# Constants of a one-core hybrid layer are given other sizes, and attention scores are issued without a wait for the low part of k

## The chip, the cores and the metric

One core of a Trainium2 chip runs the kernel. The metric is the device time of one execution in microseconds (us), as a median of several runs. The engines are TensorE (PE in the profile), VectorE (DVE), ScalarE (ACT), GpSimd (POOL) and SyncE (SP), whose queue issues most DMAs. Each works through its own instructions in program order, and semaphores hold an instruction back until its operands are there.

## The reference

A decoder layer on 512 tokens of width 2048, in float32. One input projection feeds two mixers: an RWKV-7 time mixing of 16 heads and an attention of 16 heads of 64, whose three dilated windows are mixed by their softmax denominators. Each branch is gated, then comes one output projection.

```python
h = rms_norm(x, norm_g[l])
proj = jnp.matmul(h, w_in[l]).astype(jnp.float32)
q, k, v, z_att, u_shift, z_rwkv = jnp.split(proj, splits, axis=-1)
att = dilated_mixture_attention(q, k, v, pos) * jax.nn.silu(z_att)
rwk = rwkv7_time_mix(u_shift, z_rwkv, ...) * jax.nn.silu(z_rwkv)
mix = jnp.concatenate([att, rwk], axis=-1).astype(x.dtype)
x = x + jnp.matmul(mix, w_out[l])
return rms_norm(x, final_g)
```

## The kernel before

**The main stream.** The kernel goes through items in a fixed order: the low-rank columns with `k0`; then for each of eight pairs of RWKV heads the columns r, v, z and the next k (`mm_r0`, `mm_v0`, ...); then attention's v (`mv`); q and k of four groups (`mm_qk10` to `mm_qk33`); the gates z8 to z15 (`mm_z8`, ...); at last the output projection (`mo`, `mh`, `mt`). The weights come from HBM into two raw buffers. ScalarE rounds each chunk to a high part (`whi`) and VectorE takes the rest (`wlo`); h is held as `hh` and `hl` in the same way. So every 128 rows of weights are three matmuls of 512 columns: hh by whi, hl by whi, hh by wlo. One item is 48 of them.

**Side work.** All else is written as Python generators, which issue a few instructions and yield a time or the tiles that they want to have ready. `pump` runs between the matmuls of the main stream and resumes those generators whose time has come. A planner (`Model`, `Engine`, `Queue`) keeps a clock of its own by modelled costs, and `wait_for` turns the yielded tiles into a time on it. This happens when the program is built: the result is one fixed order of instructions for each engine, and the chip knows nothing of the planner. One modelled time that moves can thus move all that is placed after it.

**Attention.** q and k of a pair of heads go through a rotation into tiles `m`, whose rows SP's queue collects by eight DMAs of 64 KB into `qa` and eight into `ka`. k is split into `kd` (ScalarE) and `kl` (VectorE). `att` works on units (a pair of heads and a quarter t of the tokens): scores `s` on TensorE (q by kd, then q by kl, for both heads), softmax on VectorE and ScalarE (`ss`, `nm`, `den`), transposes `pt` on TensorE, copied by ScalarE into `pa` and `pb`, and after the last quarter `po`, the product with v. VectorE brings po together with `yl`, the other mixers' part, which is fetched from HBM. The name of a tile counts pair, head and quarter: s400 is pair 4, head 0, quarter 0, and kl_200 belongs to group 2, first pair, head 0, which is pair 4.

**Gates.** `pg` is the product for the gate of one RWKV pair, `gh` and `gl` are its split weights, and `zz`, `zt` and `yl` on VectorE and ScalarE finish it.

**Buffers.** `k2` gives one of 20 buffers of 2 KB, `k4` one of 9 of 4 KB (q and `pa`), `small` a few columns; `cp` holds what stays for the whole kernel. A tile of a pool waits for the last reader of the tile that had the buffer before it. The constants lie below the split weights.

**Start.** `prb` on TensorE spreads the row factors of the norm, from `dg`; `rstd` and `u_lora` on VectorE follow, and the RWKV chain begins there.

Every matmul is recorded at one line, L121, every operation of the other engines at L88, every DMA at L133. So rows are told apart by tiles.

Of the kernel before, what the change touches and what calls it, by code (L numbers as in the profile page):

```python
# [11 lines left out]
F32 = mybir.dt.float32  # L12
F32R = mybir.dt.float32r
I32 = mybir.dt.int32
AF = mybir.ActivationFunctionType
ALU = mybir.AluOpType
# [4 lines left out]
P = 128  # L21
# [11 lines left out]
PV = {}  # L33
# [5 lines left out]
NPV = _o  # L39
# [97 lines left out]
def hymba_kernel(ctx: ExitStack, tc: tile.TileContext, xT, x, wa, wb, wo, pv, w2a2, g2, fg,  # L137
                 cst, rope, amask, bmask, out):
    nc = tc.nc
    ctx.enter_context(tc.manual_schedule())  # L140
    model = Model()
    V = Engine(model, nc.vector, 0.07, 0.00106, 0.18)
    S = Engine(model, nc.scalar, 0.06, 0.00095, 0.25)
# [6 lines left out]
    cp = ctx.enter_context(tc.tile_pool(name="cp", bufs=1))  # L150
    wp = ctx.enter_context(tc.tile_pool(name="wp", bufs=3))
    kp = ctx.enter_context(tc.tile_pool(name="kp", bufs=1))
# [5 lines left out]
    K1N, K2N, K4N, RAWN, AHEAD = 5, 20, 9, 2, 2  # L158

    def k2(shape, name, dt=F32):  # L160
        t = kp.tile([P, 528], dt, tag="k2", bufs=K2N, name=name)
        t = t[:, 0:math.prod(shape[1:])]
        return t if len(shape) == 2 else t.rearrange("p (a b) -> p a b", b=shape[2])

    def k1(shape, name, dt=F32):
        return kp.tile(shape, dt, tag="k1", bufs=K1N, name=name)
# [1 line left out]
    def k4(shape, name, dt=F32):  # L168
        return kp.tile(shape, dt, tag="k4", bufs=K4N, name=name)

    def ps(name, shape=(P, 512)):
        return pp.tile(list(shape), F32, tag="ps", name=name)

    def small(shape, name, bufs=12, dt=F32):
        return sp.tile(shape, dt, tag=f"s{shape[1]}", bufs=4 if shape[1] == 4 else bufs, name=name)

    pvt = cp.tile([P, 112], F32, name="pvt")
    nc.scalar.dma_start(pvt[:, 0:NPV], pv)

    def col(n, i):  # L180
        return pvt[:, PV[n] + i:PV[n] + i + 1]
# [5 lines left out]
    gmask = [csts[:, 320:448], csts[:, 448:576]]  # L187
    bmt = cp.tile([P, 2 * P], F32, name="bmt")
    ones = k2([P, P], "ones")
    V.memset(ones, 1.0)  # L190
    bonesr = cp.tile([P, P], F32R, name="bonesr")
    hw0 = cp.tile([P, 32], F32, name="hw0")
    omu = cp.tile([P, 27], F32, name="omu")
    V.tensor_scalar(omu, pvt[:, 0:27], -1.0, 1.0, ALU.mult, ALU.add)
    warm = small([P, 1], "warm")
    S.activation(warm, ones[:, 0:1], AF.Tanh)

    hth, htl, normed = [], [], []
    rstd = cp.tile([P, T], F32, name="rstd")
    rtok = cp.tile([P, 16], F32, name="rtok")[:, 0:4]  # L200
    xt_b, xq_b, Lb = [], [], []

    def prologue():
        acc = k2([P, T], "acc")
        xs = []

# [49 lines left out]
    def later():  # L256
        bones = k2([P, P], "bones")
        Q.dma_start(bones, cst[:, 576:704])
        Q.dma_start(bmt, bmask)
        yield 1.59, bones  # L260
        V.tensor_copy(bonesr, bones)
        V.tensor_scalar(hw0[:, 0:16], pvt[:, PV["w0"]:PV["w0"] + 16], 0.5, None, ALU.mult)
        V.tensor_scalar(hw0[:, 16:24], pvt[:, PV["k_a"]:PV["k_a"] + 8], -1.0, None, ALU.mult)
        for i in range(2):
            G.memset(xt_b[i], 0.0)
            G.tensor_copy(Lb[i][H[i], :, H[i]], ident[H[i], H[i]][:, None, :].to_broadcast([64, NCH, C]))
            yield 0.5, G
# [136 lines left out]
    def start(gen, *wait, rank=1):  # L404
        sides.append([gen, wait_for(*(wait or (0.0,))), rank])
# [161 lines left out]
    def spill_out(key, t):  # L567
        d = dp.tile([P, T], F32, name=f"sp_{key}")
        Q.dma_start(d, t)
        spill[key] = d  # L570
# [57 lines left out]
    def pre(p, r, k, v):  # L628
# [35 lines left out]
        a = k2([P, T], f"a{p}")  # L664
# [44 lines left out]
        V.tensor_scalar(rn2, rn2, 1e-24, None, ALU.max)  # L709
        V.reciprocal(rn2, rn2)  # L710
        start(subst(p, Mp, rn2), 0.06, Mp, rn2, rank=-1)
        S.activation(a, a, AF.Identity, bias=hw0[:, 16 + p:17 + p], scale=col("k_a", p))
        V.scalar_tensor_tensor(k, a, 1.0, k, ALU.add, ALU.mult)
        rk = k2([P, T], f"rk{p}")
        V.scalar_tensor_tensor(rk, r, col("r_k", p), k, ALU.mult, ALU.mult)
# [212 lines left out]
    def att_mask(t):  # L928
        return (am[0][:, 0:128], am[0][:, 128:384], am[1][:, 0:384], am[2])[t]
# [99 lines left out]
    def two(pa, t):  # L1029
        o = 256 if t == 3 else 0  # L1030
        return pa[:, o:o + 768].rearrange("p (j c) -> p j c", j=2)[:, :, t * P - o:t * P - o + P]

    def att(g):
        units = [(2 * g + pr_, t) for pr_ in range(2) for t in range(4)]
        po, ssb_, pts = {}, {}, {}
        for u in range(len(units) + 2):
            if u < len(units):
                pair, t = units[u]
                while pair not in ready or (t == 0 and u == 0 and pair >= 2 and pair - 1 not in scored):
                    yield 0.5  # L1040
                tl_ = pairs[pair]
                if t == 0:
                    yield 0.1, tl_["q"], tl_["kl", 0], tl_["kl", 1]
                n = max(256, 128 * (t + 1))
                nv = 128 * (t + 1)
                tsl = slice(t * P, (t + 1) * P)
                for h in range(2):
                    sc = ps(f"s{pair}{h}{t}")
                    TE.matmul(sc[:, 0:n], tl_["q"][:, h, tsl], tl_["k", h][:, 0:n], start=True, stop=False)
                    TE.matmul(sc[:, 0:n], tl_["q"][:, h, tsl], tl_["kl", h][:, 0:n], start=False, stop=True)  # L1050
                    ss = k2([P, T], f"ss{pair}{h}{t}")
                    nm = small([P, 1], f"nm{pair}{h}{t}")
                    V.tensor_tensor_reduce(ss[:, 0:nv], sc[:, 0:nv], att_mask(t), -0.125, 3.0e38,
                                           ALU.add, ALU.min, accum_out=nm)
                    den = small([P, 1], f"den{pair}{h}{t}")
                    S.activation(ss[:, 0:nv], ss[:, 0:nv], AF.Exp, bias=nm, scale=-1.0, accum_out=den)
                    ssb_[u, h] = (ss, den)
                if t == 3:
                    scored.add(pair)
            if u >= 2:  # L1060
                pair, t = units[u - 2]
                if t == 3:
                    po[pair] = pm.tile([P, T], F32, tag="mm", name=f"po{pair}")
                    for j in range(4):
                        for h in range(2):
                            hd = (2 * pair + h) * 64
                            pa, pb = pts[pair, h]
                            pj = (pa[:, 0:512], pa[:, 512:896], pb[:, 0:256], pb[:, 256:384])[j]
                            TE.matmul(po[pair][H[h], j * P:T], vt[j][:, hd:hd + 64], pj,
                                      start=(j == 0), stop=(j == 3))  # L1070
                if t == 3:
                    if f"s{pair}" in spill:
                        o = yl.pop(pair)
                        V.tensor_tensor(o, o, po.pop(pair), ALU.mult)
                    else:
                        o = k2([P, T], f"o{pair}")
                        S.copy(o, po.pop(pair))
                    spill_out(f"o{pair}", o)
                elif t == 2 and f"s{pair}" in spill:
                    fetch_y(pair, f"s{pair}")  # L1080
            if 1 <= u <= len(units):
                pair, t = units[u - 1]
                for h in range(2):
                    ss, den = ssb_.pop((u - 1, h))
                    if t == 0:
                        pts[pair, h] = (k4([P, 1024], f"pa{pair}{h}"), k2([P, T], f"pb{pair}{h}"))
                    pa, pb = pts[pair, h]
                    pt = ps(f"pt{pair}{h}{t}")
                    for j in range(t + 1):
                        TE.transpose(pt[:, j * P:(j + 1) * P], ss[:, j * P:(j + 1) * P], ident)  # L1090
                    if t == 0:
                        S.copy(pa[:, 0:P], pt[:, 0:P])
                    else:
                        S.copy(two(pa, t),
                               pt[:, 0:2 * P].rearrange("p (j c) -> p j c", j=2))
                    if t >= 2:
                        S.copy(pb[:, (t - 2) * P:(2 * t - 3) * P], pt[:, 2 * P:(t + 1) * P])
            yield 0.0, S
            if u < len(units):
                for h in range(2):  # L1100
                    ss, den = ssb_[u, h]
                    nv = 128 * (units[u][1] + 1)
                    V.reciprocal(den, den)
                    V.tensor_scalar(ss[:, 0:nv], ss[:, 0:nv], den, None, ALU.mult)
            yield 0.0, V
# [13 lines left out]
    def fetch_y(idx, key):  # L1119
        y = k2([P, T], f"yl{idx}")  # L1120
        Q.dma_start(y, spill[key])
        yl[idx] = y
# [53 lines left out]
            yield 1.05  # L1176

    fgt = []
    ssq = cp.tile([P, 4, 8], F32, name="ssq")
    yt = {}  # L1180

    def residual(nb):
# [247 lines left out]
```

## Time and profile before

| what | value |
|---|---|
| median of 3 runs | 1186.74 us (1185.92 to 1186.84) |
| profiled execution | 1185.99 us, its span 1183.9 us |
| TensorE busy | 1146.4 us, 97% of the span |
| VectorE, ScalarE, GpSimd busy | 62%, 48%, 28% |
| DMA, mean over the span | 118 GB/s, 139.62 MB |

The span runs from the first to the last instruction that the profiler recorded; the execution's own time is 2.1 us longer. TensorE's busy time counts matmuls as they follow one another. A wait of another engine costs only if TensorE waits in the end.

### The profile page before, as it was taken

To read this page: it belongs to the slowest core of one execution; us is meant where nothing else is said; L and a number is where in the kernel's file an instruction comes from. 1 tells how busy PE (TensorE), PEld (TensorE's weight loads), DVE (VectorE), ACT (ScalarE), POOL (GpSimd) and SP (SyncE) were. 2 spreads that over 40 slices of the span, in tenths; PEclk is the share of its full clock that TensorE was granted. 3 is DMA by queue.
4 is the path that set the end of the run, shared out by engine and by line. 5 is a ranking of instruction groups with operands and counts; after the bars stand their busy time and mean duration, and the time that the engine had idled before them with its cause. 6 is when DMAs were issued, how large, how long until landed. Compare 5 with 4: busy or idle time off the path is not lost. (4 is left out here: it accounts for less than half of the span.)

```text
span 1183.9 us, 19123 instructions
## 1 busy us (share of the span) xinstructions
PE 1146.4 (97%) x6878; PEld 938.2 (79%) x6878; DVE 735.2 (62%) x1511; ACT 568.6 (48%) x1254; POOL 336.4 (28%) x586
## 2 busy tenths in 40 slices
PE   7999999999999999999999999999996999999997
PEld 5788777777787777777899977777875778888897
DVE  6667887787767957768743457665655566243252
ACT  6455665645558464564433345544443445232143
POOL 1004885647328470754630001101010000011020
PEclk9999999999999999999999999999998999999999
DMA  7334333242342525234242454433452336444343
GB/s 260 118 92 130 120 105 84 84 126 84 94 136 73 139 65 151 77 100 114 59 121 59 118 166 133 132 109 116 134 142 84 116 113 213 125 125 129 103 125 143
DMA packets 89870, 139.62 MB, mean 118 GB/s; under 512 B 37936, under 2 KB 47664, under 8 KB 89776
## 3 DMA queue, kind: packets, MB, share of 16 engines
q1 hardware_dynamic: 89344, 137.83, 39.1%
q8 instruction: 54, 0.88, 0.3%
q10 hardware_dynamic: 432, 0.58, 0.1%
q14 instruction: 40, 0.33, 0.1%
HBM read 114.44 MB, written 14.75 MB: 109 GB/s over the span
## 5 line engine op out<-in xcount | busy, mean ns | idle before, releaser
L88 POOL TENSOR_TENSOR Xtmp<-XT,Mp 128x248 f32<-128x248 f32 (+30 forms) x248 | 128.9, 520 | 143.6 <-DVE XT L88 112.8
L88 POOL TENSOR_TENSOR XT<-XT,Xtmp 128x248 f32<-128x248 f32 (+30 forms) x248 | 144.6, 583 | 21.4 <-DVE XT L88 2.5
L121 PE MATMUL mm_z<-hh,wlo 128*128 128x512 f32 x256 | 104.1, 407 | 0.0
L121 PE MATMUL mm_z<-hl,whi 128*128 128x512 f32 x256 | 103.2, 403 | 0.0
L121 PE MATMUL mm_qk<-hh,whi 128*128 128x512 f32 x256 | 102.2, 399 | 0.8 <-ACT gtok L88 0.8
L121 PE MATMUL mm_qk<-hl,whi 128*128 128x512 f32 x256 | 102.8, 401 | 0.0
L121 PE MATMUL mm_z<-hh,whi 128*128 128x512 f32 x256 | 102.7, 401 | 0.0
L88 DVE TENSOR_TENSOR wlo<-raw_o,whi 128x512 fp32r<-128x512 f32 x64 | 48.0, 790 | 87.6 <-ACT whi L88 87.6
L121 PE MATMUL mm_qk<-hh,wlo 128*128 128x512 f32 x256 | 102.1, 399 | 0.0
L88 POOL TENSOR_TENSOR y<-y,fg 128x512 f32<-128x512 f32 (+1 forms) x16 | 19.3, 1237 | 272.0 <-ACT mo L88 214.1
L88 ACT ACTIVATE whi<-raw_o 128x512 fp32r<-128x512 f32 x64 | 36.8, 623 | 96.5 <-PE mo L121 73.2
L88 POOL TENSOR_TENSOR m<-m,m 128x512 f32<-128x512 f32 x16 | 22.9, 1451 | 197.7 <-DVE m L88 92.5
L88 ACT ACTIVATE ss<-ss,nm 128x128 f32<-128x128 f32 (+3 forms) x64 | 35.5, 556 | 87.0 <-DVE nm L88 87.0
L121 PE MATMUL mo<-whi,ml 128*128 128x512 f32 x192 | 75.8, 395 | 0.0
L121 PE MATMUL mo<-whi,mh 128*128 128x512 f32 x192 | 75.8, 395 | 0.0
L121 PE MATMUL mo<-wlo,mh 128*128 128x512 f32 x192 | 75.8, 395 | 0.0
L88 DVE TENSOR_TENSOR wlo<-raw_v,whi 128x352 fp32r<-128x352 f32 (+1 forms) x80 | 50.3, 655 | 35.2 <-ACT whi L88 33.9
L88 DVE TENSOR_TENSOR wlo<-raw_z,whi 128x512 fp32r<-128x512 f32 x64 | 48.1, 771 | 33.2 <-ACT whi L88 32.9
L88 DVE TENSOR_TENSOR wlo<-raw_qk,whi 128x512 fp32r<-128x512 f32 x64 | 46.5, 745 | 32.2 <-ACT whi L88 32.1
L121 PE MATMUL mv<-whi,hh 128*128 128x352 f32 x192 | 62.7, 327 | 1.5 <-DVE m L88 1.5
L88 ACT ACTIVATE whi<-raw_v 128x352 fp32r<-128x352 f32 (+1 forms) x80 | 40.8, 542 | 46.5 <-PE mv L121 33.5
L121 PE MATMUL mv<-wlo,hh 128*128 128x352 f32 x192 | 62.2, 324 | 0.0
(303 smaller groups left out, 3043.8 us busy)
## 6 DMA issues: line engine op xcount, KB each, us to landing
raw_z<-in_wa_dram SPq DMA_DIRECT2D x32, 512.0 KB
raw_qk<-in_wa_dram SPq DMA_DIRECT2D x32, 512.0 KB
raw_o<-in_wo_dram SPq DMA_DIRECT2D x32, 512.0 KB
raw_v<-in_wb_dram SPq DMA_DIRECT2D x24, 352.0 KB
raw_r<-in_wa_dram SPq DMA_DIRECT2D x16, 512.0 KB
raw_v<-in_wa_dram SPq DMA_DIRECT2D x16, 512.0 KB
raw_k<-in_wa_dram SPq DMA_DIRECT2D x15, 512.0 KB
xk<-in_xT_dram SPq DMA_DIRECT2D x16, 256.0 KB
```

Of the source, the lines that this page charges most:

```text
L88: return fn(o, *args, **kw)
L121: return fn(o, lhs, rhs, **kw)
```

## The change

Three things are edited. The buffers of `k2` become 2080 bytes apart instead of 2112 (a tile of the wanted shape is returned directly), and some constants are cut to what is used: `pvt` from 112 to 99 columns, `hw0` from 32 to 16, `rtok`, `ssq`; `warm` moves to the constants. The negated k_a gets a tile of its own, `nka`, of 256 bytes; before, it lay in columns 16 to 23 of `hw0`. Together these put the split weights at 115584 instead of 115456 bytes. And in `att` the wait ahead of a pair's first scores, for q and both `kl`, is taken out.

```diff
     def k2(shape, name, dt=F32):
-        t = kp.tile([P, 528], dt, tag="k2", bufs=K2N, name=name)
-        t = t[:, 0:math.prod(shape[1:])]
-        return t if len(shape) == 2 else t.rearrange("p (a b) -> p a b", b=shape[2])
+        return kp.tile(shape, dt, tag="k2", bufs=K2N, name=name)
...
-    pvt = cp.tile([P, 112], F32, name="pvt")
-    nc.scalar.dma_start(pvt[:, 0:NPV], pv)
+    pvt = cp.tile([P, NPV], F32, name="pvt")
+    nc.scalar.dma_start(pvt, pv)
...
-    hw0 = cp.tile([P, 32], F32, name="hw0")
+    hw0 = cp.tile([P, 16], F32, name="hw0")
+    nka = cp.tile([P, 64], F32, name="nka")
...
-    warm = small([P, 1], "warm")
+    warm = cp.tile([P, 1], F32, name="warm")
...
-    rtok = cp.tile([P, 16], F32, name="rtok")[:, 0:4]
+    rtok = cp.tile([P, 4], F32, name="rtok")
...
-        V.tensor_scalar(hw0[:, 0:16], pvt[:, PV["w0"]:PV["w0"] + 16], 0.5, None, ALU.mult)
-        V.tensor_scalar(hw0[:, 16:24], pvt[:, PV["k_a"]:PV["k_a"] + 8], -1.0, None, ALU.mult)
+        V.tensor_scalar(hw0, pvt[:, PV["w0"]:PV["w0"] + 16], 0.5, None, ALU.mult)
+        V.tensor_scalar(nka[:, 0:8], pvt[:, PV["k_a"]:PV["k_a"] + 8], -1.0, None, ALU.mult)
...
-        S.activation(a, a, AF.Identity, bias=hw0[:, 16 + p:17 + p], scale=col("k_a", p))
+        S.activation(a, a, AF.Identity, bias=nka[:, p:p + 1], scale=col("k_a", p))
...
                 tl_ = pairs[pair]
-                if t == 0:
-                    yield 0.1, tl_["q"], tl_["kl", 0], tl_["kl", 1]
                 n = max(256, 128 * (t + 1))
...
-    ssq = cp.tile([P, 4, 8], F32, name="ssq")
+    ssq = cp.tile([P, 4, 5], F32, name="ssq")
```

With the last edit, and with `nka` as a tile of its own, the planner's times differ, and with them the order on every engine. Three places show what that means.

The first is on TensorE, at the first scores of pair 4 (s400, s410) in the second item of group 3, whose matmuls are mm_qk31; the number behind hh is the block of 128 rows of h, 0 to 15. Before:

```order
L121 MATMUL mm_qk31_8630<-hh11_198,wlo119_8577 128x512
L121 MATMUL mm_qk31_8630<-hh12_204,whi119_8576 128x512
L121 MATMUL mm_qk31_8630<-hl12_205,whi119_8576 128x512
L121 MATMUL s400_8710<-kd_200_8667,q_20_8349 128x256
L121 MATMUL s400_8710<-kl_200_8668,q_20_8349 128x256
L121 MATMUL s410_8718<-kd_201_8671,q_20_8349 128x256
L121 MATMUL s410_8718<-kl_201_8672,q_20_8349 128x256
L121 MATMUL mm_qk31_8630<-hh12_204,wlo119_8577 128x512
```

Now:

```order
L121 MATMUL mm_qk31_8631<-hl7_164,whi118_8489 128x512
L121 MATMUL mm_qk31_8631<-hh7_163,wlo118_8490 128x512
L121 MATMUL s400_8681<-kd_200_8668,q_20_8351 128x256
L121 MATMUL s400_8681<-kl_200_8669,q_20_8351 128x256
L121 MATMUL s410_8689<-kd_201_8672,q_20_8351 128x256
L121 MATMUL s410_8689<-kl_201_8673,q_20_8351 128x256
L121 MATMUL mm_qk31_8631<-hh8_169,whi119_8577 128x512
```

The four rows stand behind 24 matmuls of mm_qk31, where they stood behind 38. At the place of s000 they stand 11 matmuls earlier than before. What VectorE has ahead of kl_200 is the same in both: the additions to yl, two m, two q, two wlo.

The second is on VectorE, ahead of kl_100 and kl_101, which the first scores of pair 2 (s200, s210) read. Before:

```order
L88 TENSOR_TENSOR wlo111_7941<-raw111_qk21_7776,whi111_7940 128x512 x2
L88 RECIPROCAL den103_7917<-den103_7917 128x1
L88 TENSOR_SCALAR ss103_7914<-ss103_7914,den103_7917 128x512
L88 RECIPROCAL den113_7925<-den113_7925 128x1
L88 TENSOR_SCALAR ss113_7922<-ss113_7922,den113_7925 128x512
L88 TENSOR_TENSOR kl_100_7976<-ka_100_7893,kd_100_7975 128x512
L88 TENSOR_TENSOR kl_101_7980<-ka_101_7898,kd_101_7979 128x512
```

Now:

```order
L88 TENSOR_TENSOR wlo111_7956<-raw111_qk21_7815,whi111_7955 128x512 x2
L88 TENSOR_TENSOR yl1_7964<-yl1_7964,po1_7994 128x512
L88 TENSOR_TENSOR m0_20_8012<-mm_qk20_7830,L0_234 128x512
L88 TENSOR_TENSOR m3_20_8014<-mm_qk20_7830,L0_234 128x512
L88 TENSOR_TENSOR q_11_8016<-qa_110_7923,q_11_8016 64x512
L88 TENSOR_TENSOR q_11_8016<-qa_111_7928,q_11_8016 64x512
L88 TENSOR_TENSOR wlo112_8026<-raw112_qk22_7886,whi112_8025 128x512 x2
L88 TENSOR_TENSOR kl_100_8047<-ka_100_7933,kd_100_8046 128x512
L88 TENSOR_TENSOR kl_101_8051<-ka_101_7938,kd_101_8050 128x512
```

The addition to yl1, which needs po1 and a fetch from HBM, now stands ahead of the two kl, and so do the rows of m, q and wlo. On SP the eight qa DMAs of that group now stand ahead of the eight ka DMAs, and the fetch of yl1 behind them. On TensorE s200 stands behind 24 matmuls of mm_qk21, where it stood behind 19.

The third is on TensorE in the gate stage, around po5. Before, the transposes pt600 and pt610 come first, and po5 stands 39 matmuls behind them:

```order
L121 MATMUL mm_z9_9294<-hl11_199,whi127_9180 128x512
L121 MATMUL s601_9387<-kd_300_9203,q_30_9008 128x256
L121 MATMUL s601_9387<-kl_300_9204,q_30_9008 128x256
L121 MATMUL s611_9395<-kd_301_9207,q_30_9008 128x256
L121 MATMUL s611_9395<-kl_301_9208,q_30_9008 128x256
L121 MATMUL pt600_9405<-csts_82,ss600_9281 128x128
L121 MATMUL pt610_9410<-csts_82,ss610_9289 128x128
```

Now po5 comes ahead even of the first scores of pair 6:

```order
L121 MATMUL po5_9343<-pb50_9047,vt3_6099 64x128
L121 MATMUL po5_9343<-pb51_9052,vt3_6099 64x128
L121 MATMUL mm_z9_9280<-hh8_169,whi127_9223 128x512
L121 MATMUL mm_z9_9280<-hl8_170,whi127_9223 128x512
L121 MATMUL mm_z9_9280<-hh8_169,wlo127_9224 128x512
L121 MATMUL mm_z9_9280<-hh9_181,whi127_9223 128x512
L121 MATMUL mm_z9_9280<-hl9_182,whi127_9223 128x512
L121 MATMUL s600_9360<-kd_300_9332,q_30_8973 128x256
```

pt600 stands 32 rows behind the end of po5, and the four matmuls of pg2 directly behind pt610. At the start of the program, prb stands behind 42 matmuls of v0 and has six behind it, where it stood behind all 48.

## Rows read from the trace of the kernel before

**Rows 1.** The page: busy time, share, instructions; granted clock in 40 slices.

```profile
PE 1146.4 (97%) x6878; PEld 938.2 (79%) x6878; DVE 735.2 (62%) x1511; ACT 568.6 (48%) x1254; POOL 336.4 (28%) x586
...
PEclk9999999999999999999999999999998999999999
```

**Rows 2.** TensorE's waits: who is waited for, us in total, times, longest.

```profile
PE pt L121 <- DVE den L88: 5.4, 3, 3.7
PE pg L121 <- DVE nm L88: 5.0, 1, 5.0
PE zpb L121 <- DVE xnb L88: 2.7, 2, 1.7
...
PE mm_k L121 <- DVE u_lora L88: 1.6, 1, 1.6
...
PE s L121 <- DVE kl L88: 1.0, 2, 0.7
...
PE pt L121 <- DVE yl L88: 0.9, 2, 0.7
```

**Rows 3.** Windows of the gate stage: length, busy by engine (instructions), PEclk, DMA.

```profile
890.38:892.13 1.75, 0.00 (x0) 0.03 (x1) 1.68 (x6) 1.56 (x3) 0.00 (x0) 0.50 0.52 150
892.13:897.20 5.07, 5.07 (x19) 4.67 (x20) 4.43 (x13) 2.05 (x7) 0.00 (x0) 0.50 0.46 152
897.20:908.10 10.90, 10.90 (x53) 7.76 (x52) 0.00 (x0) 1.29 (x6) 0.00 (x0) 1.00 0.01 3
...
914.27:917.40 3.13, 0.00 (x0) 0.03 (x1) 3.07 (x9) 0.13 (x2) 0.00 (x0) 0.50 0.46 103
917.40:921.10 3.70, 3.70 (x9) 2.93 (x10) 1.83 (x6) 2.91 (x9) 0.00 (x0) 0.50 0.34 127
```

**Rows 4.** Timeline, TensorE, gate stage: start, us, operation, [idle before <- releaser].

```profile
878.05 0.55 PE L121 MATMUL pt<-csts,ss 128*128 128x128 f32 x3 [0.73 <-DVE yl L88]
...
892.13 1.94 PE L121 MATMUL pt<-csts,ss 128*128 128x128 f32 x8 [3.73 <-DVE den L88]
...
910.62 0.87 PE L121 MATMUL pt<-csts,ss 128*128 128x128 f32 x4 [0.72 <-DVE den L88]
...
917.40 0.76 PE L121 MATMUL pg<-g128h,gh 128*128 128x512 f32 x1 [4.98 <-DVE nm L88]
...
918.39 0.63 PE L121 MATMUL pg<-g128h,gl 128*128 128x512 f32 x1
918.82 0.63 PE L121 MATMUL pg<-g32s,gl 128*128 128x512 f32 x1
```

**Rows 5.** Timelines, VectorE (first three rows) and TensorE, around prb.

```profile
52.18 0.87 DVE L88 TENSOR_SCALAR dg<-csts,rtok 128x128 f32<-128x128 f32 x4
...
57.12 0.69 DVE L88 COPY rstd<-prb 128x512 f32<-128x512 f32 x1 [3.47 <-PE prb L121]
...
57.84 0.69 DVE L88 TENSOR_TENSOR u_lora<-mm_lora,rstd 128x512 f32<-128x512 f32 x1
...
56.06 1.02 PE L121 MATMUL prb<-dg,ones 128*128 128x512 f32 x2
58.68 0.47 PE L121 MATMUL mm_k<-hh,whi 128*128 128x512 f32 x1 [1.60 <-DVE u_lora L88]
```

**Rows 6.** Timeline, TensorE: first and last of two unbroken runs of matmuls.

```profile
820.20 0.39 PE L121 MATMUL mm_qk<-hl,whi 128*128 128x512 f32 x1
...
827.87 0.39 PE L121 MATMUL mm_qk<-hl,whi 128*128 128x512 f32 x1
...
898.64 0.40 PE L121 MATMUL mm_z<-hh,whi 128*128 128x512 f32 x1
...
905.15 0.40 PE L121 MATMUL mm_z<-hl,whi 128*128 128x512 f32 x1
```

**Rows 7.** Timelines of VectorE and ScalarE in the gate stage.

```profile
887.81 0.69 DVE L88 TENSOR_TENSOR zz<-mm_z,rstd 128x512 f32<-128x512 f32 x1 [4.67 <-DMA ka<-m]
...
907.29 0.27 ACT L88 COPY pa<-pt 128x128 f32<-128x128 f32 x1 [9.61 <-PE po L121]
```

**Rows 8.** Timelines of VectorE (kl) and TensorE (s) at s000 and s200.

```profile
699.73 0.69 DVE L88 TENSOR_TENSOR kl<-ka,kd 128x512 fp32r<-128x512 f32 x1 [1.80 <-ACT kd L88]
...
700.48 0.39 PE L121 MATMUL s<-kl,q 128*128 128x256 f32 x1 [0.36 <-DVE kl L88]
...
757.70 1.29 DVE L88 TENSOR_TENSOR kl<-ka,kd 128x512 fp32r<-128x512 f32 x2
...
761.58 0.28 PE L121 MATMUL s<-kd,q 128*128 128x256 f32 x1
```

**Rows 9.** Timelines of SP, VectorE and TensorE at s400.

```profile
810.13 4.95 SPq L133 DMA_DIRECT2D qa<-m  x8
...
821.14 0.58 SPq L133 DMA_DIRECT2D yl<-sp_s  x1
...
824.56 0.69 DVE L88 TENSOR_TENSOR yl<-yl,po 128x512 f32<-128x512 f32 x1 [7.91 <-DMA yl<-sp_s]
...
829.01 1.28 DVE L88 TENSOR_TENSOR kl<-ka,kd 128x512 fp32r<-128x512 f32 x2
...
828.80 0.28 PE L121 MATMUL s<-kd,q 128*128 128x256 f32 x1
829.74 0.39 PE L121 MATMUL s<-kl,q 128*128 128x256 f32 x1 [0.66 <-DVE kl L88]
```

## The prediction

> **What bounds the kernel now.** I read the page's busy times first. TensorE is busy for 97% of the span and VectorE for 62% [rows 1], so only what TensorE waits for, and the rate at which it is clocked, can move the time. Then the waits of TensorE: the five groups that matter here hold 5.4, 5.0, 1.6, 1.0 and 0.9 us [rows 2], 13.9 of the 37.5 us of the span in which it is not busy (1183.9 - 1146.4). Then the stretches by clock [rows 3]: the granted clock is 1.00 (2.4 GHz) except for two pieces late in the gate stage, 890.38 to 897.20 and 914.27 to 921.10, where it is 0.50 (1.2 GHz). Each begins inside one of the two longest waits, 3.73 and 4.98 us [rows 4], and after each of them TensorE works on at half clock, for 5.07 and 3.70 us. The wait of 1.60 us at 58.68 [rows 5] did not lower the clock: the page's slice there, the second of forty, has a 9 [rows 1].
>
> What one matmul of 512 columns costs: from the start at 820.20 to that at 827.87 there are 33 steps, and from 898.64 to 905.15 there are 28 [rows 6], 0.2324 and 0.2325 us each. At half clock two of them start 0.43 us apart (918.39, 918.82) [rows 4]. So each microsecond at half clock loses 1 - 0.232/0.43 = 0.46 us; the two pieces lost 2.3 and 1.7 us.
>
> **What the edits themselves cost.** Addresses: the built programs have the same number of matmuls, and no instruction is made longer. The split weights lie 128 bytes higher; the k2 buffers lie 2080 instead of 2112 bytes apart. In the trace TensorE keeps one step in two stages, with weights that rotate through three buffers and sixteen parts of h at as many offsets [rows 6]; I take 0. The bounds: a change of the step by 0.6 ns (a quarter of a percent, about what two such pairs of rows could hide) would be 3 us over 1146 us of TensorE [rows 1], up or down. The smaller tiles and `nka` cost nothing: the same instructions write them. But the planner no longer sees the second VectorE write wait for the first one's tile, and that shifts its clock by 0.1 us, so from row 149 of TensorE's program on the side work is placed anew. What counts, then, is the order.
>
> **The first place: prb.** Before, `prb` stands behind all 48 matmuls of v0, and TensorE waits 1.60 us for `u_lora`, which VectorE makes from `prb` (57.12 and 57.84) [rows 5]. Now six v0 matmuls stand behind it, 6 x 0.232 = 1.39 us. `dg`, which `prb` needs, is written from 52.18 on, 3.9 us before `prb` starts at 56.06, so it can go 1.4 us earlier: **-1.4 us**.
>
> **The tail.** Two stalls feed the long waits. VectorE sat 4.67 us before `zz` at 887.81 for the ka DMAs: `zz8` got a k2 buffer whose last reader was a ka DMA issued just before it. Behind `zz` stood the den that releases `pt` at 892.13. And ScalarE sat 9.61 us before a `pa` copy at 907.29, until `po` on TensorE ended: pa61 reuses pa50, which po5 reads, and po5 stood 39 matmuls behind pt610 [rows 7]. Behind that copy stood split weights and gates, so that `pg` came at 917.40. In the changed program po5 stands 32 rows ahead of pt600, and zz8's buffer belonged to a kl tile that scores read long before. So both waits go, 3.73 + 4.98 us [rows 4], and with them the 0.72 at 910.62 and the 0.73 at 878.05 that belong to the same units [rows 4]: **-10.2 us**. Without the two waits the clock stays up: 2.3 + 1.7, **-4.0 us**.
>
> **The removed wait.** Without it, the four matmuls of a pair's first scores are put into TensorE's queue whatever the state of `kl`; TensorE runs in order, so all that is behind them waits too: the projection, whose weights are ready.
>
> s000 stands 11 matmuls earlier. In the trace it already waits: `kl` for the second head begins at 699.73 and the last s matmul starts at 700.48 after 0.36 us [rows 8]. Nothing on VectorE, ScalarE or SP makes `kl` earlier, so the whole 11 x 0.232 is added: **+2.6 us**. TensorE would come to it at about 697.0 and be through at 700.5.
>
> s400 stands 14 matmuls earlier, with the same rows ahead of `kl` on VectorE and on SP. The chain there is [rows 9]: SP issues eight qa and eight ka DMAs (810.13 to 821.1), then the fetch of yl at 821.14; VectorE sits 7.91 us for it until 824.56, and `m`, `q`, `wlo` and then both `kl` stand behind it in its queue, 829.01 to 830.29. In the trace s400 starts at 828.80 and then waits 0.66 us for kl. From 14 x 0.232 = 3.25 us earlier the wait is about 4.0 us, and the net is **+3.3 us**.
>
> s200 had no wait: both `kl` were done at 757.70 + 1.29 = 758.99, ahead of s at 761.58 [rows 8]. In the changed order VectorE has the yl addition, two `m`, two `q` and two `wlo` ahead of kl_100, and SP has qa ahead of ka and the fetch of yl behind them, which is the pattern of s400 to the row. s200 stands behind 24 matmuls of its group, as s400 does. I price it by s400: **+4.0 us**.
>
> The two waits of about 4.0 us lie between the 3.73 and the 4.98 that came with a half clock. I take one piece of half clock for each at the mean of the two seen, 2 x 2.0: **+4.0 us**. In the Trainium skill, "TensorE: Matmul & The Clock Gate", section "Why this matters for your kernels", a stream of matmuls is to be kept free of idle gaps of some microseconds, because the clock falls back to half; the two falls here, with 3.73 and 4.98 us of idling ahead, agree. The rule speaks against this change: by it s000's broken wait of some 3.3 us may bring a third fall, and the sum would be 2.0 us higher.
>
> s600 is the third of this kind that moves: it now stands right behind po5. On VectorE nothing of the fetch of yl stands ahead of its `kl`, though zz8 and yl9 do. In the changed order some 19 us of matmuls lie between the load of z10's weights, behind which its DMAs stand on SP, and s600; s400's chain took 830.29 - 810.13 = 20.2 us [rows 9]; as the fetch (821.14 to 824.56, 3.4 us) is not in it, I take **+0.5 us**; the ends are 0 and a full wait with its clock, 4.0 + 2.0. The rest of the RWKV half is dealt anew, about as often closer as farther: 0, with 2.5 us either way, about what xnb's two waits there come to, 2.7 us [rows 2].
>
> **The sum.** -1.4 - 10.2 - 4.0 + 2.6 + 3.3 + 4.0 + 4.0 + 0.5 = -1.2 us, against the profiled execution's 1185.99 us (span 1183.9): 1184.8. The median shown is 1186.74, 0.75 higher, so I give **1185.5 us**.
>
> **The rivals.** (1) The score waits are cheap. If both waits leave the clock at 1.00, 4.0 us fall away: 1181.5; if s200 also finds its kl ready, as it did before, another 4.0: 1177.5; the middle is about 1180. For it speaks that 4.0 is close to 3.73 and that no wait between 1.7 and 3.7 us stands in [rows 2]. Against it: VectorE's queue is the one that made s400 late. (2) Slower, by one mechanism: s600 waits as s400 does. If VectorE reaches zz8 or yl9 late, kl_300 is late by up to 4.0 us and the clock falls with it, 6.0 instead of 0.5: 1191.0. For it speaks that the same engines made s400 late, against it that no fetch is in its chain. It decides from the point at which that chain takes more than the 19 us of cover by over 2 us. (3) The tail keeps its stalls: pg2 in the changed order takes the PSUM buffer of s601, which stands directly ahead of it, and if VectorE is as far behind as it was, half of the 14.2 us stays: 1192.6. For it: VectorE was idle only because of DMAs that are still issued. Against: po5 is out of the way. (4) The addresses alone change TensorE's step: 1182.5 to 1188.5 by the bound above. The trace shows nothing for it. (5) That the change does nothing, because the scores are not on the path, is excluded by the 1.0 us that s already waits [rows 2].
>
> **The numbers.** A run of this kernel tells from no change about 0.2%, 2.4 us. The forecast has 0.40, its own range 1182.5 to 1188.5 by the RWKV half; rival 1 has 0.25, rival 2 0.20, rival 3 0.07, rival 4 0.08. Below 1184.4 lie about 0.11 of the forecast, 0.23 of rival 1 and 0.02 of rival 4: faster 0.36. Above 1189.1 lie 0.02, 0.01, 0.16, 0.07 and 0.00: slower 0.26. The rest, 0.38, is no change. The range 1179 to 1192 leaves out the end of rival 1 in which s200 finds its kl ready (0.09) and, above, rival 3 and the last of rival 2 (0.10).
>
> **What would show it.** In the profile after: no wait of u_lora by mm_k over 0.3 us; no wait of pt for den or of pg over 1 us late in the gate stage, and clock 1.00 there; s waiting for kl at three places, about 3, 4 and 4 us, with a half clock after at least two; steps of 0.232 us. The prediction is wrong if s200 and s400 wait for under 2 us, if s600 waits for over 2, or if the step is another.

## The result, and the profile after

The changed kernel takes 1168.01 us (median of 4 runs, 1166.51 to 1169.49), the kernel before 1186.33 beside it; the ratio is 0.9847, 95% interval 0.9828 to 0.9867. That is 18.3 us less, and lies below the range of the prediction.

The page of the changed kernel, busy time and granted clock, to be read against [rows 1]:

```profile
PE 1135.5 (97%) x6878; PEld 940.4 (81%) x6878; DVE 736.4 (63%) x1524; ACT 561.7 (48%) x1241; POOL 338.0 (29%) x586
...
PEclk9999999999999999999999999999899999999999
```

TensorE has as many matmuls as before and is busy for 10.9 us less. The other engines' busy times move by 1.2 to 6.9 us. The slice with a lower clock has moved from the gate stage to the one around s400.

TensorE's waits, to be read against [rows 2]:

```profile
PE s L121 <- DVE kl L88: 7.6, 4, 4.2
...
PE s L121 <- ACT kd L88: 1.6, 2, 1.3
PE zpb L121 <- DVE xnb L88: 0.9, 1, 0.9
...
PE mm_k L121 <- DVE u_lora L88: 0.2, 1, 0.2
...
PE pg L121 <- DVE nm L88: 0.2, 1, 0.2
```

The two long waits of the gate stage are gone (pt for den is no longer in the list, pg has 0.2 us), and s has 9.2 us where it had 1.0. Here they are in TensorE's timeline: s000, s200 and s400.

```profile
690.83 0.38 PE L121 MATMUL s<-kd,q 128*128 128x256 f32 x1 [0.21 <-ACT kd L88]
691.55 0.38 PE L121 MATMUL s<-kl,q 128*128 128x256 f32 x1 [0.34 <-DVE kl L88]
693.28 0.39 PE L121 MATMUL s<-kd,q 128*128 128x256 f32 x1 [1.35 <-ACT kd L88]
694.07 0.58 PE L121 MATMUL s<-kl,q 128*128 128x256 f32 x1 [0.40 <-DVE kl L88]
...
763.81 0.39 PE L121 MATMUL s<-kl,q 128*128 128x256 f32 x1 [2.70 <-DVE kl L88]
...
828.62 0.58 PE L121 MATMUL s<-kl,q 128*128 128x256 f32 x1 [4.16 <-DVE kl L88]
```

VectorE's timeline at s400 shows the chain that the prediction took over from [rows 9]: the addition to yl waits 8.01 us for its fetch, and kl stands behind.

```profile
823.44 0.69 DVE L88 TENSOR_TENSOR yl<-yl,po 128x512 f32<-128x512 f32 x1 [8.01 <-DMA yl<-sp_s]
...
827.89 1.28 DVE L88 TENSOR_TENSOR kl<-ka,kd 128x512 fp32r<-128x512 f32 x2
```

The windows at those places (length, busy PE, PEld, DVE, ACT, POOL, PEclk, DMA), and the whole gate stage in the last row:

```profile
693.67:697.09 3.42, 3.02 (x8) 2.44 (x9) 0.85 (x5) 1.55 (x5) 0.00 (x0) 0.50 0.63 187
765.35:768.77 3.42, 3.42 (x10) 2.68 (x9) 2.01 (x6) 1.35 (x4) 0.00 (x0) 0.50 0.76 212
826.79:828.62 1.83, 0.00 (x0) 0.00 (x1) 1.83 (x4) 0.00 (x0) 0.00 (x0) 0.50 0.00 0
828.62:833.62 5.00, 5.00 (x13) 4.02 (x14) 3.15 (x11) 2.03 (x6) 0.00 (x0) 0.50 0.75 195
866.00:982.70 116.70, 116.54 (x566) 94.00 (x565) 75.27 (x175) 53.28 (x142) 2.99 (x2) 1.00 0.49 149
```

At each of the three score waits the granted clock stands at 0.50 in this execution, and TensorE worked on at it for 3.02, 3.42 and 5.00 us, which at the prediction's 0.46 lost per us is 1.4, 1.6 and 2.3 us. A fourth piece, 24.66 to 28.07, lies at the program's start, where TensorE waits for weights; E3, which has the same order there, has none. In the gate stage TensorE is busy for 116.54 of 116.70 us at full clock.

So far that is the forecast. What it did not have is in the output projection, where TensorE does nothing but matmuls of 512 columns, without a wait in either kernel. The same window, first of the kernel before, then of the changed one:

```profile
1010.00:1110.00 100.00, 100.00 (x432) 81.04 (x432) 34.52 (x46) 26.71 (x53) 11.02 (x8) 1.00 0.39 117
```

```profile
1010.00:1110.00 100.00, 100.00 (x443) 82.84 (x442) 33.15 (x46) 27.24 (x54) 11.50 (x8) 1.00 0.38 116
```

11 more matmuls fit into the same 100 us at the same clock. The step has become shorter. In the z15 columns, unbroken by side work, 36 steps lie between these two starts of the changed kernel, 8.16 / 36 = 0.2267 us each, where [rows 6] have 0.2324 (the windows count also what is under way at their ends):

```profile
974.57 0.39 PE L121 MATMUL mm_z<-hh,wlo 128*128 128x512 f32 x1
...
982.73 0.39 PE L121 MATMUL mm_z<-hh,wlo 128*128 128x512 f32 x1
```

### The profile page after: what moved, and what is told of

The parts are those of the page before. It is cut to its first block, busy times and chain, and to the rows that moved or that the text cites. A ratio compares the mean times of both kernels' runs of the same rounds, so it can differ in the third digit from the quotient of the medians.

```text
span 1167.6 us, 19121 instructions
## 1 busy us (share of the span) xinstructions
PE 1135.5 (97%) x6878; PEld 940.4 (81%) x6878; DVE 736.4 (63%) x1524; ACT 561.7 (48%) x1241; POOL 338.0 (29%) x586
## 5 line engine op out<-in xcount | busy, mean ns | idle before, releaser
L88 POOL TENSOR_TENSOR Xtmp<-XT,Mp 128x248 f32<-128x248 f32 (+30 forms) x248 | 132.8, 536 | 170.0 <-DVE XT L88 152.7
L88 POOL TENSOR_TENSOR XT<-XT,Xtmp 128x248 f32<-128x248 f32 (+30 forms) x248 | 142.2, 573 | 21.4 <-DVE XT L88 2.5
L121 PE MATMUL mv<-whi,hl 128*128 128x352 f32 x192 | 62.8, 327 | 0.0
```

The lines of the kernel that those rows point to most:

```text
L88: return fn(o, *args, **kw)
L121: return fn(o, lhs, rhs, **kw)
```

## The experiments

Theory A: the place of the split weights sets TensorE's step. Theory B: the new order does, by what runs beside it. Rival C: the distance of the k2 buffers does.

**E1. The order of before, the addresses of after.**

```diff
-        t = kp.tile([P, 528], dt, tag="k2", bufs=K2N, name=name)
+        t = kp.tile([P, 520], dt, tag="k2", bufs=K2N, name=name)
-    pvt = cp.tile([P, 112], F32, name="pvt")
+    pvt = cp.tile([P, 144], F32, name="pvt")
```

> The kernel before, every engine's order unchanged; pvt is 128 bytes longer and k2 buffers are 2080 bytes apart, so the split weights lie at 115584 and the rest as in the change. Theory A (the place of the split weights sets TensorE's step): steps of 226 to 228 ns instead of 232.5 over some 3400 matmuls of 512 columns, so about 1171 us, with the old waits of 3.7 and 5.0 us still there. Theory B (the new order sets the step, by what runs beside it): 232.5 ns and 1186 us.

1177.06 us against 1186.96 on the same chip, ratio 0.992 (0.9905 to 0.9934). The window of the output projection has 443 matmuls, as in the change:

```profile
1010.00:1110.00 100.00, 100.00 (x443) 82.81 (x442) 32.10 (x44) 26.44 (x53) 11.52 (x8) 1.00 0.39 120
```

The old waits are still there:

```profile
PE pt L121 <- DVE den L88: 6.2, 4, 3.9
...
PE pg L121 <- DVE nm L88: 5.0, 1, 5.0
```

B falls as the account of the shorter step, which comes without the new order. The gain is 9.9 us and not the 15.5 that the expectations took. In the profiled execution TensorE is busy for 1134.9 us, 11.5 less than in [rows 1], and idle for 2.1 us more, some of it in waits on chains of VectorE, which TensorE now reaches sooner (for xnb 3.6 us in all, where [rows 2] have 2.7). Behind the longest of these, 1.96 us, stand 3.41 us of half clock that the kernel before has not there, some 1.6 us lost. The rest was not followed.

**E1c. Only the k2 distance.** The first two lines of that diff alone.

> The kernel before with k2 buffers 2080 instead of 2112 bytes apart and nothing else; split weights stay at 115456, order unchanged. Theory A: 232.5 ns and 1186 us. Rival C (the distance of the k2 buffers sets the step): 227 ns and about 1171 us.

1186.94 us, ratio 0.9997 (0.9988 to 1.0006). C falls: the k2 distance costs and brings nothing.

**E2. The order of after, the split weights back at 115456.**

```diff
-    nka = cp.tile([P, 64], F32, name="nka")
+    nka = cp.tile([P, 32], F32, name="nka")
```

> The changed kernel with nka of 128 instead of 256 bytes, so the split weights are back at 115456; order unchanged. Theory A: steps of 232.5 ns and 1168 + 15.5 = about 1183.5 us. Theory B: 227 to 228 ns and 1168 us.

1179.22 us, ratio 0.9936 (0.992 to 0.9953). The window has 430 matmuls:

```profile
1010.00:1110.00 100.00, 100.00 (x430) 80.42 (x429) 33.24 (x44) 26.19 (x52) 11.04 (x8) 1.00 0.37 113
```

So the address is worth 11.2 us in the new order (by the medians; 10.6 by the ratios to the kernel before), 9.9 in the old, and the order without the address 7.7 us.

**E3. The change with the wait put back.**

```diff
+                if t == 0:
+                    yield 0.1, tl_["q"], tl_["kl", 0], tl_["kl", 1]
```

> The changed kernel with the wait ahead of a pair's first scores put back; addresses as changed. Theory A: steps of 226 to 228 ns; the waits of s for kl and kd (9.2 us) and the half clocks after them (about 5 us) go, other waits of this order come; 1158 to 1170 us. If the score waits had been what made the kernel faster: over 1175 us.

1171.41 us, ratio 0.9875 (0.9859 to 0.989). Against E1, which has the same k2 distance and the same place of the split weights, what is left is the new tile `nka` with what it does to the planner's times, and the smaller items (`warm` moved, tiles cut), which no run parts from it: 5.6 us less. TensorE's waits, of E1 first:

```profile
PE zpb L121 <- DVE xnb L88: 3.6, 2, 2.0
...
PE mm_k L121 <- DVE u_lora L88: 1.6, 1, 1.6
PE mv L121 <- DVE m L88: 1.5, 1, 1.5
PE pM L121 <- DVE bt L88: 1.2, 2, 0.8
PE pb L121 <- DVE l_rk L88: 1.1, 1, 1.1
```

and of E3:

```profile
PE pg L121 <- DVE nm L88: 5.0, 1, 5.0
...
PE zpb L121 <- DVE xnb L88: 0.9, 1, 0.9
...
PE mm_k L121 <- DVE u_lora L88: 0.2, 1, 0.2
```

These 9.0 us of waits became 1.1 (mv, pM and pb are no longer in the list), while TensorE's waits for the tile A, also of that half, rose from 2.1 to 4.1 us. In the profiled executions E3 is idle for 2.8 us less than E1. The clock has a part in the difference too: TensorE works for 12.50 us at half clock in E1 and for 6.73 in E3, which at 0.46 is 2.7 of the 4.8 us between their spans. Only the piece behind xnb goes with a wait that the new order shortened; the waits of the tail are as long in both (3.9 and 5.0 us) and have half clocks of different length behind them. So the 5.6 us are not all the order's. The long waits of the gate stage are still in E3 (pt for den up to 3.9, pg 5.0): it is the removed wait, not `nka`, that clears the tail. Between E3 and the change lie 3.4 us by the medians, measured beside different runs of before (ratios 0.9875 and 0.9847).

**E4 to E8. Which place.** A tile's place is the byte address at which it starts in a partition; what counts below is its remainder modulo 256. In the kernel before all parts of h lie at 128 mod 256, and the split weights at 0. Of a matmul's two operands the stationary one has an instruction of its own that loads it, LDWEIGHTS in the trace; the other is the moving one, and the rows name it first. In the projections (`mm_`) the weights are stationary and h moves, in the output projection (`mo`) the parts of the mixed result, which lie in h's buffers, are stationary and the weights move. Two theories on the pair: A1, h and the weights must have the same place; A2, the weights must not lie at 0. All four have the order of before and k2 at 2080; E4 and E5 put 128 bytes ahead of h and of the constants (E4's edit is shown without its k2 line), E5 takes them out of the constants again, E6 and E8 lengthen pvt.

```diff
+    hpad = hp.tile([P, 32], F32, name="hpad")
     cp = ctx.enter_context(tc.tile_pool(name="cp", bufs=1))
```

> The kernel before with k2 at 2080 and 128 bytes ahead of the constants: the parts of h (hh, hl) lie at 16640 (0 mod 256), the split weights at 115584 (128 mod 256). Order unchanged. Theory A1 (what counts is that h and the split weights have the same place mod 256): unequal, so steps of 232.5 ns and about 1187 us. Theory A2 (what counts is that the split weights are not at 0 mod 256, whatever h is): 227 to 228 ns and about 1177 us.

> As the run before it, with the constants cut by 128 bytes: h at 16640 and the split weights at 115456, both at 0 mod 256. Order unchanged. Theory A1: equal, so 227 to 228 ns and about 1177 us. Theory A2: 232.5 ns and about 1187 us.

> The kernel before with k2 at 2080 and pvt 64 bytes longer: h at 16512 (128 mod 256), split weights at 115520 (64 mod 256). Theory A1, if places must be equal: 232.5 ns and 1187 us. Theory A2: 227 to 228 ns and 1177 us. Something between would say that the distance counts by degrees.

> The kernel before with k2 at 2080 and pvt 192 bytes longer: h at 16512 (128 mod 256), split weights at 115648 (192 mod 256). Theory A1: 232.5 ns and 1187 us. Theory A2: 227 to 228 ns and 1177 us.

| run | h mod 256 | weights mod 256 | weights less h | matmuls in the window | us |
|---|---|---|---|---|---|
| before | 128 | 0 | 128 | 432 | 1185.8 to 1187.06 |
| E1 | 128 | 128 | 0 | 443 | 1177.06 |
| E4 | 0 | 128 | 128 | 432 | 1186.93 |
| E5 | 0 | 0 | 0 | 443 | 1174.82 |
| E6 | 128 | 64 | -64 | 430 | 1182.13 |
| E8 | 128 | 192 | 64 | 438 | 1185.94 |

E4 to E8 are single runs, beside a run of before of 1185.8. E5 decides: with the weights at 0 as before, and h moved to 0, the step is the short one, and with both moved (E4) it is the long one. Their windows, E4 first:

```profile
1010.00:1110.00 100.00, 100.00 (x432) 81.06 (x431) 34.08 (x46) 27.34 (x54) 11.03 (x8) 1.00 0.39 119
```

```profile
1010.00:1110.00 100.00, 100.00 (x443) 82.81 (x442) 33.39 (x46) 27.12 (x54) 11.51 (x8) 1.00 0.38 116
```

A2 falls. A1 holds for equal and for opposite places. E1 lengthens the distance from h to the weights by 128 bytes and E5 shortens it by 128, with the same 443: so the remainder by 256 is enough. Between equal and opposite it is not all or nothing. In E6 the projections, where h moves and lies 64 bytes above the stationary weights (mod 256), take 0.2288 us (42 steps from 982.92 to 992.53); the output projection, where the weights move, 64 bytes below the stationary operand, has 430:

```profile
982.92 0.39 PE L121 MATMUL mm_z<-hh,wlo 128*128 128x512 f32 x1
...
992.53 0.39 PE L121 MATMUL mm_z<-hh,wlo 128*128 128x512 f32 x1
```

```profile
1010.00:1110.00 100.00, 100.00 (x430) 80.56 (x429) 33.22 (x44) 25.93 (x52) 11.02 (x8) 1.00 0.39 120
```

In E8, with the sign turned, it is the other way about. The projections take the long step, 0.2333 us (49 steps from 984.34 to 995.77), and the output projection is the better one (438):

```profile
984.34 0.39 PE L121 MATMUL mm_z<-hh,whi 128*128 128x512 f32 x1
...
995.77 0.39 PE L121 MATMUL mm_z<-hl,whi 128*128 128x512 f32 x1
```

```profile
1010.00:1110.00 100.00, 100.00 (x438) 82.06 (x437) 33.08 (x46) 27.27 (x54) 11.56 (x8) 1.00 0.41 125
```

So in these two runs the sign of the distance between the moving and the stationary operand counts: 64 bytes above costs about a third of the difference between the short and the long step, 64 bytes below all of it.

**E9 and E10. Which of the removed waits.** Theory D: s400's early place alone rearranges the tail, the other two only cost. E9 puts the wait back for pairs 0 and 2, E10 for pair 4.

```diff
+                if t == 0 and (pair in (0, 2)):
+                    yield 0.1, tl_["q"], tl_["kl", 0], tl_["kl", 1]
```

> The changed kernel with the wait put back for pairs 0 and 2 alone (s000 and s200 stand at their old places, s400 at its new one, po5 ahead of pt600 as in the change). Theory D (the early s400 alone rearranges the tail; early s000 and s200 only cost): the waits at s000 and s200 (2.3 and 2.7 us) and their half clocks (about 1.5 us each) go, the tail stays free: 1160 to 1163 us. Rival E (the tail is freed by all three moves together, or the stalls only move): 1168 us or more.

> The changed kernel with the wait put back for pair 4 alone (s400 back at its old place, s000 and s200 at their new ones; po5 39 matmuls behind pt610 again). Theory D: the wait of 4.2 us at s400 becomes 0.7 and its half clock goes, but the tail's waits of 3.8 and 5.0 us and their half clocks are back: 1168 - 3.5 - 2.3 + 10.2 + 4.0 = about 1176 us. Rival E: at or below 1168 us.

E9: 1160.92 us, ratio 0.9774 (0.9758 to 0.9791), the fastest kernel here. E10: 1176.34 us, ratio 0.9909 (0.9894 to 0.9924). TensorE's waits, of E9 and then of E10:

```profile
PE s L121 <- DVE kl L88: 4.4, 2, 4.0
...
PE pt L121 <- DVE den L88: 1.9, 3, 1.3
...
PE pg L121 <- DVE nm L88: 0.2, 1, 0.2
```

```profile
PE pg L121 <- DVE nm L88: 5.0, 1, 5.0
PE pt L121 <- DVE den L88: 4.2, 2, 3.5
PE s L121 <- DVE kl L88: 3.9, 4, 2.8
```

In E9 s400's 4.0 us is left and the two long waits of the tail are gone. In E10 they are back. D holds as far as pairs 0, 2 and 4 go; the waits of the other pairs are out in both runs. The early s000 and s200 cost 1168.0 - 1160.9 = 7.1 us by the medians (8.7 by the ratios); the waits taken out at the other pairs bring E3 to E9, 10.5 us (12.0 by the ratios).

**E11 and E12. Is there a better place?** nka of 56 and of 72 columns in the changed kernel, so the weights lie 32 bytes below and above h's place.

> The changed kernel with nka of 224 bytes: the split weights lie 32 bytes lower (96 mod 256, h at 128), order unchanged. If only equal places give 226.7 ns: 229 to 233 ns and 1172 to 1180 us. If the step grows with the distance on the one side and falls on the other (matmuls of 256 columns took 113.5 instead of 119.5 ns with the weights 64 bytes below h): under 226.7 ns for qk and z, over for the output projection, and about 1168 us.

> The changed kernel with nka of 288 bytes: split weights 32 bytes higher (160 mod 256, h at 128), order unchanged. With a sign to the distance: over 230 ns for qk and z, and the output projection, which reads h's buffers as the moving operand, nearer to 226; about 1177 us.

1180.21 and 1177.54 us in single runs, both with 430 matmuls in the window, E11 first:

```profile
1010.00:1110.00 100.00, 100.00 (x430) 80.50 (x429) 33.22 (x44) 26.20 (x52) 11.02 (x8) 1.00 0.38 116
```

```profile
1010.00:1110.00 100.00, 100.00 (x430) 80.36 (x429) 33.21 (x44) 26.19 (x52) 11.02 (x8) 1.00 0.38 115
```

The last z columns have 0.2333 us in both. The guess that a step of 32 bytes to the one side helps was wrong: both roles are slow on both sides. (E12's expectation also has the roles the wrong way round: in the output projection h's buffers hold the stationary operand.) The equal place gives the shortest step of 512 columns among the six distances tried.

## Why the prediction was wrong

**The step that failed** is "In the trace TensorE keeps one step in two stages, with weights that rotate through three buffers and sixteen parts of h at as many offsets [rows 6]; I take 0." The step was measured rightly, but the offsets were no sample: buffers of 4096 bytes and parts of h 2048 bytes apart all have the same place mod 256, h at 128 and the weights at 0. The trace before held one distance, 128, and could not speak on another. The bound of 3 us was the scatter of the rows and had nothing to do with what an address could do. Rival 4 named the mechanism and was given that same bound; it is worth 9.9 us (E1) to 11.2 us (E2). Of the prediction's own three signs of being wrong, "if the step is another" is the one that came.

**"The rest of the RWKV half is dealt anew, about as often closer as farther: 0".** With prb's 1.4 the sum had 1.4 us from `nka`; E3 less E1 is 5.6. u_lora's wait fell to 0.2 us as forecast. The waits for xnb, bt, l_rk and m fell by 6.5 us and those for A rose by 2.0; a part of the 5.6 is the clock, as said at E3. Why the new places of just those are better was not followed further.

**The tail** was right in its mechanism: po5 ahead of pt600, both long waits gone, the clock up. The forecast was 14.2 us. s400's early place, which brings the new tail, was to cost 3.3 us and a half clock of 2.0, s600 0.5: -8.4 us in sum. E9 less E3 gives -10.5 (-12.0 by the ratios). In the other direction E10 was expected at 1176 and came at 1176.34.

**The score waits.** At s400 4.16 us, forecast 4.0. At s200 2.70, forecast 4.0: its chain, from the first qa DMA to the end of the second kl, takes 18.7 us (745.64 to 764.36) where s400's takes 20.2 (809.02 to 829.17); SP's eight ka DMAs alone take 4.96 us there and 6.20 at s400. At s000 the four waits sum to 2.3 us, of which 0.36 stood there before; the forecast was 2.6 more. s600 does not wait, forecast 0.5. The half clocks cost 5.3 us by the windows, forecast 4.0: a third came at s000, as was said to be possible. That is one execution: in E2, of the same order, the clock stays at 1.00 behind the 2.40 us at s200, and in E11 behind the four waits at s000, so the term has no fixed size. By runs, s000 and s200 with their half clocks were 2.6 + 4.0 + 2.0 = 8.6 us in the forecast and are 7.1 (E9). That the wait of 1.60 us left the clock up was read from a 9 in a slice of 29.6 us, which cannot show it: the changed kernel's slice with 3.42 us of half clock at s000 has a 9 too. The window itself (58.68 to 62.10 of the kernel before) has 1.00, so the reading was right.

**In sum**, in two steps of the same order: the addresses -9.9, `nka` -5.6, the removed wait -3.4, which is 18.9 by medians beside 1186.96 (the change itself was timed beside 1186.33). The forecast had 0, -1.4 and +0.2. Each is a difference of medians of a few runs, with half clocks that come and go in it; ten runs of one kernel (E1c) span 2.4 us. Most of the miss is the addresses; rival 1 (cheap score waits), whose time of 1177 to 1181 lies nearer, would have been wrong in its reason.

## What to carry to other kernels

A steady step of TensorE that is longer than it need be shows in no wait and no share of busy time; count matmuls in a window without waits, and when every operand has the same address modulo some power of two, one trace says nothing on another address: shift one pool by 64 or 128 bytes and look. Where a planner at build time sets the order, a wait is two things, a stall and a place in the order: taking it out made three stalls of 2 to 4 us and removed two of 4 to 5 us, and putting it back one pair at a time kept the gain without most of the cost.

## What the runs showed that was not expected

A matmul of 512 columns in fp32r takes 0.2267 us in an unbroken run (443 in 100 us) when the stationary and the moving operand start at the same place mod 256, and 0.2324 (432; 430 in E2) when they are 128 bytes apart, whichever of the two is shifted (E1, E2, E4, E5). With 32 bytes between them it is the long step on both sides (430). What in the chip makes the step longer, and why E2 has 430 and not 432, no run shows.

Matmuls of other widths go another way. The 576 of 352 columns (`mv`) hold TensorE for 96.78 us in the kernel before and in E1 alike. Of 256 columns, the mh part took 22.37 us for 192 with the weights 64 bytes below (E6), and 23.56 us with equal places (the changed kernel):

```profile
1127.10:1149.70 22.60, 22.37 (x192) 21.98 (x193) 0.81 (x3) 0.31 (x1) 1.00 0.43 135
```

```profile
1113.50:1137.20 23.70, 23.56 (x192) 23.12 (x192) 0.82 (x3) 0.32 (x1) 1.00 0.41 130
```

The clock fell behind shorter waits than the 3.73 and 4.98 us of the kernel before, but not every time. In the changed kernel it stood at 0.50 behind one wait of 2.70 us (s200) and around four waits of 2.3 us together (s000). In E2 it stayed at 1.00 behind 2.40 us at s200, and in E11 around the four waits at s000 (2.2 us). Around the waits for xnb it fell in E1 (1.96 us) and even in E1c (1.44 us), and stayed up in the kernel before (1.65 us). The windows of E2, E11 and E1c:

```profile
769.36:773.36 4.00, 3.90 (x17) 3.12 (x18) 2.57 (x11) 2.03 (x6) 0.00 (x0) 1.00 0.74 214
```

```profile
699.30:703.30 4.00, 4.00 (x18) 3.26 (x19) 1.12 (x5) 2.15 (x6) 0.00 (x0) 1.00 0.56 148
```

```profile
169.63:173.04 3.41, 3.41 (x39) 2.40 (x38) 3.38 (x6) 2.71 (x7) 3.10 (x5) 0.50 0.39 124
```

So in these runs the length of a wait alone does not tell whether the clock falls behind it, and an order's price in half clocks is read from several executions, not from one.
